# A two-layer encoder kernel: merging the delta rule's chunk stores and moving the load of its decay rows

## The chip, the core and the metric

The kernel runs on one core of a Trainium2 chip. The metric is the device time of one execution in microseconds (us). The core has five engines that run at the same time, each with its own instruction stream in a fixed order: TensorE (PE in the profile, with PEld for its weight loads), VectorE (DVE), ScalarE (ACT), GpSimd (POOL) and SyncE (SP). Here SP issues nearly all the transfers (DMAs) between the device memory (DRAM) and the on-chip memory. An instruction whose input is not there holds up everything behind it on its engine.

## The reference, cut to what matters

The reference runs a two-layer encoder on two sequences, `x_prompt` of 2048 tokens ("p" in the kernel's names) and `x_sample` of 1024 tokens ("s"). Each layer projects the normalised input, runs four mixers side by side (attention, gated delta rule, gated linear attention, attention over a memory), and projects their outputs back. The change touches the gated delta rule, which runs forwards and backwards over chunks of 64 tokens:

```
qkv = jax.nn.silu(short_conv_centered(d_qkv, gdn_conv_w))
qb, kb, vb = jnp.split(qkv, 3, axis=-1)
qb, kb, vb = l2_norm(heads(qb, HEAD_DIM)), l2_norm(heads(kb, HEAD_DIM)), heads(vb, HEAD_DIM)
...
b = jnp.cumsum(g, axis=-1)
diff = b[..., :, None] - b[..., None, :]
decay = jnp.where(incl, jnp.exp(jnp.where(incl, diff, 0.0)), 0.0)
kk = jnp.einsum('bhnid,bhnjd->bhnij', k, k)
lower = jnp.where(strict, beta[..., :, None] * kk * decay, 0.0)
t_mat = lower + jnp.eye(CHUNK, dtype=jnp.float32)
sol = lax.linalg.triangular_solve(t_mat, rhs, left_side=True, lower=True)
...
def step(state, inp):
    qd, a, u_c, w_c, kd, cd = inp
    v_new = u_c - jnp.einsum('bhcd,bhde->bhce', w_c, state)
    o = jnp.einsum('bhcd,bhde->bhce', qd, state) + jnp.einsum('bhij,bhje->bhie', a, v_new)
    state = cd[..., None, None] * state + jnp.einsum('bhcd,bhce->bhde', kd, v_new)
    return state, o
```

## The kernel before

**Streams.** `run` merges generators. A main stream holds the projections (`proj`, `outproj`) in the first and third part of the program and attention plus gated linear attention in the others; a side stream, `right`, goes through the delta rule (`gdn`) of both sequences and layers, and through some of the mixers of the short sequence. `merge` always takes the next step from the stream whose clock stands lowest, where each `yield` says what its step counts (7000 for a chunk tile, 5200 for a projection's tile). A scheduler of the framework then orders the instructions of each engine by priority and by its own model of the chip, so the order on every engine is fixed when the kernel is built.

**The delta rule.** Groups of 1024 tokens go through `gdn_rows` (decay sums and gates, written to the DRAM tensor `rows`), `gdn_chunks`, `gdn_inv` (inverse of the 32 by 32 diagonal blocks, on VectorE) and, when the sequence's groups are through, `gdn_scan`. There are six groups in the program: one a layer of the short sequence, two a layer of the long one. The change is in `gdn_chunks` and in the two that read what it stores.

**`gdn_chunks`.** A group has four blocks of 256 tokens with two tiles of 128 each: 24 blocks and 48 tiles in all. A block first makes v, q and k (the loop over `m`): `raw` is loaded, convolved into `c`, passed through silu with `e`, and for q and k normalised by way of the matmul at L749, `y` and `u`; the result is `qk`. Then each tile

- loads `rb`, the decay and gate rows, copied to 64 partitions at a time (two DMAs of 256 KB, as pieces of 512 bytes),
- copies k into the block-diagonal `kbd` (ScalarE), multiplies k with k and q (L776), and transposes k and v (L779, L780),
- makes `eb = exp(rb)` on ScalarE (L144 is the helper's line, so tile names tell the instructions apart), `dt` from `rb` and `eb` on GpSimd and ScalarE, and from them the pieces of `cm` and `lt`, the lower triangle,
- stores `cm` (one DMA of 772 KB to `cmb`), and `lt` in twelve DMAs of 16 KB: eight with the 32 by 32 diagonal blocks to `lu`, four with the blocks that join them to `off`.

**Buffers.** A tile with two buffers can be written while the last one is still being read; with one buffer the next writer waits. Before, `rb`, `dt`, `eb`, `lt`, `cm`, `e` and `y` have two each, `u` one.

**SP.** All loads and stores of all streams stand in SP's one order. What the projections need (`whi` and `wlo`, 1 MB of weights each) stands in it between the chunks' loads and stores.

Of the kernel before, what the change touches and what calls it, by code (L numbers as in the profile page):

```python
# [16 lines left out]
P = 128  # L17
# [18 lines left out]
HALF = 32  # L36
# [34 lines left out]
class Kern:  # L71
# [641 lines left out]
    def gdn_chunks(self, X, L, g, pp):  # L713
        nc, I = self.nc, self.I
        wide = 2
        with self.tc.tile_pool(name=self.nm("gc"), bufs=1, side="right") as cp:
            mk = lambda shape, tag, bufs=1: self.t(cp, shape, tag, bufs=bufs)
# [3 lines left out]
            for x in kbds:  # L721
                nc.gpsimd.memset(x, 0.0)
            for b in range(g * 1024, g * 1024 + 1024, 256):
                qk = mk([P, 2, 2, 256], "qk", 2)
                vT = mk([P, 2, 256], "vT", 2)
                for m in range(3):
                    raw = mk([P, 2, 258], "raw", 2)
# [8 lines left out]
                    c, e = mk([P, 2, 256], "c", 2), mk([P, 2, 256], "e", wide)  # L736
                    for h in range(2):
                        w = lambda i: cw[:, m * 2 + h, i:i + 1]
# [10 lines left out]
                    nc.tensor.matmul(out=ps, lhsT=self.blk, rhs=e)  # L749
                    y, u = mk([P, 2, 256], "y", wide), mk([P, 2, 256], "u")  # L750
                    self.act(y, ps, AF.Ln, bias=self.eps)
# [3 lines left out]
                    f = 0.125 if m == 0 else 1.0  # L755
# [3 lines left out]
                    yield 4500  # L759
                for tt in range(2):  # L760
                    T = b // P + tt
                    rb = mk([P, 2, 2, 2, P], "rb", wide)
                    kbd = kbds[T % 2]
                    for i in range(2):
                        r = slice(i * 64, i * 64 + 64)
                        self.copy(kbd[r, :, :, r], qk[r, :, 0, tt * P:(tt + 1) * P].rearrange("p h (c t) -> p h c t", c=2))
                    for i in range(2):
                        r = X.rows[g, i].rearrange("w (d h c) t -> (w d h) (c t)", d=2, h=2)[:, (T % 8) * P:(T % 8) * P + P]
                        self.ld(rb[i * 64:i * 64 + 64].rearrange("p w d h x -> p (w d h) x"), r.partition_broadcast(64))
                    rows = lambda w, d: rb[:, w, d].rearrange("p h (c t) -> p c h t", c=2)  # L770
# [7 lines left out]
                    for hp in range(2):  # L778
                        nc.tensor.transpose(out=ptk[:, 0, hp], in_=qk[:, hp, 0, tt * P:(tt + 1) * P], identity=self.ident)  # L779
                        nc.tensor.transpose(out=ptk[:, 1, hp], in_=vT[:, hp, tt * P:(tt + 1) * P], identity=self.ident)  # L780
                    cm = mk([P, 1544], "cm", 2)
                    kv = cm[:, 516:1028].rearrange("p (a c h t) -> p a c h t", a=2, c=2, h=2)
                    for c in range(2):
                        for i in range(2):
# [3 lines left out]
                            else:  # L788
                                nc.vector.tensor_copy(out=o, in_=x)
                    dt, lt, eb = mk([P, 2, 4, 64], "dt", wide), mk([P, 2, 4, 64], "lt", 2), mk([P, 2, 2, 2, 64], "eb", wide)  # L790
                    self.act(eb.rearrange("p d h c t -> p d h (c t)"), rb[:, 0], AF.Exp)
# [14 lines left out]
                    self.st(X.cmb[T], cm)  # L806
                    lu = X.lu[T // 8].rearrange("(d x i) (p j t) -> d i p x j t", d=2, i=2, p=2, j=HALF)
                    x0 = (T % 8) * 4
                    for i in range(2):
                        for p in range(2):  # L810
                            r = slice(i * 64 + p * HALF, i * 64 + p * HALF + HALF)
                            for d in range(2):
                                self.st(lu[d, i, p, x0:x0 + 4].rearrange("x j t -> j x t"), lt[r, d, :, p * HALF:p * HALF + HALF])
                            self.st(X.off[T, p, i], lt[r, p, :, (1 - p) * HALF:(1 - p) * HALF + HALF])
                    yield 7000

    def gdn_inv(self, X, g):

        nc = self.nc
        with self.tc.tile_pool(name=self.nm("gi"), bufs=1, side="right") as ip:  # L820
            fl = lambda x: x.rearrange("p q a b -> p (q a b)")
            U, Y = (self.t(ip, [P, 2, HALF, HALF], n) for n in "UY")
            tmp = self.t(ip, [P, 2 * (HALF // 2) ** 2], "t")
            self.ld(fl(U)[0:64], X.lu[g][0:64])
            self.ld(fl(Y)[64:128], X.lu[g][64:128])
            self.copy(fl(U)[64:128], fl(Y)[64:128, ::-1])
            nc.gpsimd.memset(Y, 0.0)
            nc.gpsimd.memset(Y.rearrange("p q a b -> p q (a b)")[:, :, ::HALF + 1], 1.0)
            for b in range(HALF - 1, 0, -1):
                w = HALF - b  # L830
                t = tmp[:, 0:2 * b * w].rearrange("p (q a c) -> p q a c", q=2, c=w)
                self.vtt(t, b_last(U[:, :, 0:b, b], w), b_at(Y[:, :, b, b:], 2, b), ALU.mult)
                self.vtt(Y[:, :, 0:b, b:], Y[:, :, 0:b, b:], t, ALU.subtract)
                yield 400 + 4 * b * w
            self.copy(fl(U)[64:128], fl(Y)[64:128, ::-1])
            self.st(X.xt[g][0:64], fl(Y)[0:64])
            self.st(X.xt[g][64:128], fl(U)[64:128])
            yield 1500
# [22 lines left out]
    def gdn_scan(self, X, pp):  # L861
        nc = self.nc
        NT = X.S // P
        with self.tc.tile_pool(name=self.nm("gs"), bufs=1, side="right") as cp:
# [14 lines left out]
            def prep(d, T, it):  # L879
                g, x0 = T // 8, (T % 8) * 4  # L880
                cm = mk([P, 1028], "cm", SB_)
                self.ld(cm, X.cmb[T][:, d * 516:d * 516 + 1028])
                cd, qd, at, kv = ((0, 4, 260, 516), (1024, 768, 512, 0))[d]
                v4 = lambda o: cm[:, o:o + 256].rearrange("p (x t) -> p x t", x=4)
                xt = X.xt[g].rearrange("(d x i) (p j t) -> d i p x j t", d=2, i=2, p=2, j=HALF)
                xb, nb = xtb[it % SB_], nbd[d]
                for i in range(2):
                    for p in range(2):
                        r = slice(i * 64 + p * HALF, i * 64 + p * HALF + HALF)
                        self.ld(xb[r, :, r], xt[d, i, p, x0:x0 + 4].rearrange("x j t -> j x t"))  # L890
                    a, o = i * 64 + d * HALF, i * 64 + (1 - d) * HALF
                    self.ld(nb[a:a + HALF, :, o:o + HALF], X.off[T, d, i])
                kvi, ka = mk([P, 4, P], "kvi", KB_), mk([P, 4, P], "ka", KA)
# [178 lines left out]
    def seq(self, nm, S, x, y, mc0):  # L1072
        X = Seq()
        X.nm, X.S, X.x, X.y, X.mc0, X.delta_ready, X.mixed, X.units_done = nm, S, x, y, mc0, (-1, 0), set(), 0
        NT, NG = S // P, S // 1024
        for n, shape in (("h", (S, D)), ("qT", (256, S)), ("kT", (P, S)), ("v", (S, P)), ("gaT", (256, S)), ("mqT", (256, S)),
                         ("gmT", (256, S)), ("dT", (768, S)), ("halo", (1, 768)), ("gd", (S, 256)), ("lqkT", (256, S)), ("lv", (S, 256)),
                         ("gl", (S, 256)), ("smT", (NG, 48, 1024)), ("yT", (D, S)), ("rows", (NG, 2, 2, 64, 64)),
                         ("cmb", (NT, P, 1544)), ("lu", (NG, P, 2048)), ("xt", (NG, P, 2048)), ("off", (NT, 2, 2, HALF, 4, HALF))):
            setattr(X, n, self.dram(nm + n, shape))  # L1080
        return X
# [163 lines left out]
```

## Time and profile before

| what | us |
|---|---|
| median of 3 runs | 5534.79 (5528.48 to 5540.68) |
| the profiled execution, its own time | 5524.39 |
| its span, first to last instruction | 5522.6 |
| TensorE busy in it | 4762.8 (86%) |
| VectorE, ScalarE, GpSimd busy | 3184.6, 2287.8, 1862.9 |
| `gdn_chunks` runs in | 215 to 430, 1337 to 1545, 1632 to 1830, 2300 to 2540, 3698 to 3890, 4120 to 4316 |

The busy time of an engine counts its arithmetic, not its waits. TensorE's clock is granted by the chip at one of two levels, 2.4 GHz (1.00 in the rows) or 1.2 GHz (0.50); a mean between them says how the stretch was shared. Of the six stretches of chunks, the fourth lies beside attention, the others beside projections.

### The profile page before, as it was taken

To read this page: it belongs to the slowest core of one execution; us is meant where nothing else is said; L and a number is where in the kernel's file an instruction comes from. 1 tells how busy PE (TensorE), PEld (TensorE's weight loads), DVE (VectorE), ACT (ScalarE), POOL (GpSimd) and SP (SyncE) were. 2 spreads that over 40 slices of the span, in tenths; PEclk is the share of its full clock that TensorE was granted. 3 is DMA by queue.
4 is the path that set the end of the run, shared out by engine and by line. 5 is a ranking of instruction groups with operands and counts; after the bars stand their busy time and mean duration, and the time that the engine had idled before them with its cause. 6 is when DMAs were issued, how large, how long until landed. Compare 5 with 4: busy or idle time off the path is not lost. (4 is left out here: it accounts for less than half of the span.)

```text
span 5522.6 us, 76962 instructions
## 1 busy us (share of the span) xinstructions
PE 4762.8 (86%) x26984; PEld 3660.2 (66%) x26984; DVE 3184.6 (58%) x6175; ACT 2287.8 (41%) x5027; POOL 1862.9 (34%) x1836
## 2 busy tenths in 40 slices
PE   6878999899678798578889899986887899999998
PEld 5758888667576698434455478665865866555887
DVE  4465254554556525577876665626426478877553
ACT  4344233434425244454444433424325255554332
POOL 0232121043413323266656220324104234665222
PEclk8989999999888899778999999998988999999999
DMA  5556343433575544332222246334534543232674
GB/s 188 165 175 200 117 136 129 141 110 123 158 228 159 194 154 114 79 92 56 72 67 74 72 165 212 109 109 116 188 117 123 171 130 94 62 94 56 244 261 152
DMA packets 558154, 746.61 MB, mean 135 GB/s; under 512 B 227200, under 2 KB 420486, under 8 KB 528584
## 3 DMA queue, kind: packets, MB, share of 16 engines
q1 hardware_dynamic: 557768, 741.69, 42.8%
q8 instruction: 214, 3.51, 0.3%
q14 instruction: 172, 1.41, 0.1%
HBM read 490.41 MB, written 251.07 MB: 134 GB/s over the span
## 5 line engine op out<-in xcount | busy, mean ns | idle before, releaser
L278 PE MATMUL b<-whi,xhi 128*128 128x256 f32 x3520 | 1017.2, 290 | 65.1 <-ACT stg L147 34.4
L278 PE MATMUL b<-wlo,xhi 128*128 128x256 f32 x3520 | 1012.1, 288 | 0.0
L278 PE MATMUL b<-whi,xlo 128*128 128x256 f32 x3520 | 1004.6, 288 | 0.1
L153 POOL TENSOR_TENSOR acc<-acc,p 128x512 f32<-128x512 f32 x544 | 738.0, 1357 | 419.9 <-ACT p L144 386.4
L278 PEld LDWEIGHTS b<-whi,xhi 128*128 128x128 f32 x3520 | 685.5, 195 | 100.4 <-issue 40.1
L278 PEld LDWEIGHTS b<-whi,xlo 128*128 128x128 f32 x3520 | 680.9, 195 | 23.5 <-issue 14.7
L278 PEld LDWEIGHTS b<-wlo,xhi 128*128 128x128 f32 x3520 | 685.5, 195 | 16.3 <-issue 12.4
L565 DVE TENSOR_REDUCE mx<-b 128x1 f32<-128x512 f32 (+1 forms) x832 | 501.8, 622 | 287.4 <-PE b L564 283.5
L278 PE MATMUL b<-xhi,whi 128*128 128x512 f32 x1472 | 598.0, 407 | 51.9 <-DMA whi<-hi_wg 23.0
L278 PE MATMUL b<-xlo,whi 128*128 128x512 f32 x1472 | 591.8, 402 | 0.6 <-DVE xlo L150 0.6
L144 ACT ACTIVATE p<-b 128x512 f32<-128x512 f32 x736 | 417.4, 595 | 419.3 <-PE b L635 402.5
L278 PE MATMUL b<-xhi,wlo 128*128 128x512 f32 x1472 | 589.7, 401 | 0.0
L634 PE MATMUL b<-qh,kst 128*128 128x512 f32 x736 | 345.2, 471 | 48.7 <-DVE mx L565 36.3
L564 PE MATMUL b<-kst,qh 128*128 128x512 f32 (+1 forms) x832 | 342.5, 443 | 41.6 <-ACT p L144 25.5
L278 PEld LDWEIGHTS b<-xhi,whi 128*128 128x128 f32 x1472 | 278.8, 189 | 138.3 <-ACT stg L147 28.2
L621 PE MATMUL b<-p,vst 128*64 128x512 f32 x1280 | 361.3, 635 | 3.9 <-ACT p L144 3.7
L278 PEld LDWEIGHTS b<-xhi,wlo 128*128 128x128 f32 x1472 | 277.1, 188 | 78.3 <-issue 13.2
L278 PEld LDWEIGHTS b<-xlo,whi 128*128 128x128 f32 x1472 | 278.5, 189 | 73.9 <-issue 9.4
L635 PE MATMUL b<-qlm,kh 68*128 68x512 f32 x736 | 299.6, 420 | 19.4 <-DVE qlm L150 19.1
L634 PEld LDWEIGHTS b<-qh,kst 128*128 128x128 f32 x736 | 145.0, 197 | 219.3 <-DVE mx L565 99.4
L564 PEld LDWEIGHTS b<-kst,qh 128*128 128x128 f32 x832 | 159.6, 200 | 174.5 <-ACT p L144 65.7
L147 ACT ACTIVATE stg<-b 128x512 f32<-128x512 f32 (+2 forms) x212 | 112.7, 545 | 322.9 <-PE b L278 240.9
(249 smaller groups left out, 9152.3 us busy)
## 6 DMA issues: line engine op xcount, KB each, us to landing
whi<-hi_wg SPq DMA_DIRECT2D x48, 1024.0 KB
wlo<-lo_wg SPq DMA_DIRECT2D x48, 1024.0 KB
cm<-pcmb SPq DMA_DIRECT2D x64, 514.0 KB
whi<-hi_wout SPq DMA_DIRECT2D x28, 1024.0 KB
wlo<-lo_wout SPq DMA_DIRECT2D x28, 1024.0 KB
pcmb<-cm SPq DMA_DIRECT2D x32, 772.0 KB
h<-in_wg_dram SPq DMA_DIRECT2D x48, 512.0 KB
hi_wg<-whi SPq DMA_DIRECT2D x24, 1024.0 KB
```

The source lines that it names most:

```text
L144: self.nc.scalar.activation(out=out, in_=in_, func=func, **k)
L147: self.nc.scalar.activation(out=out, in_=in_, func=AF.Copy)
L153: self.nc.gpsimd.tensor_tensor(out=out, in0=a, in1=b, op=op)
L278: self.nc.tensor.matmul(out=out, lhsT=a, rhs=b, start=(i == 0), stop=(i == len(terms) - 1))
L564: nc.tensor.matmul(out=ps, lhsT=qh[:, qt * P:(qt + 1) * P], rhs=kst[:, lb * LB:(lb + 1) * LB])
L565: nc.vector.tensor_reduce(out=mx[:, qt, lb:lb + 1], in_=ps, axis=AX.X, op=ALU.max)
L621: return nc.tensor.matmul(out=pv[r], lhsT=vst[:, lt, 0:64], rhs=p, start=(lt < 2), stop=(lt >= NL - 2))
L634: nc.tensor.matmul(out=s, lhsT=kst[:, lt * P:(lt + 1) * P], rhs=qh, start=True, stop=False)
L635: nc.tensor.matmul(out=s, lhsT=kh1[0:68, lt * P:(lt + 1) * P], rhs=qlm[0:68], start=False, stop=True)
```

## The change

Each chunk tile stores five pieces instead of thirteen. `lt` becomes the last 512 columns of `cm`, so that the joining blocks go out with the store of `cm` (1028 KB) and the scan reads them from `cmb`; the tensor `off` goes. The order of the lanes in `lu` and `xt` is changed so that one store of 32 KB (256 pieces of 128 bytes) takes a diagonal block of both directions, four stores a tile. `rb` is loaded for both tiles at the head of its block, ahead of `raw`, and has three buffers; to make room, `y` and `eb` go from two buffers to one.

```
@@ gdn_chunks
+            def rb_load(T):
+                rb = mk([P, 2, 2, 2, P], "rb", 3)
+                for i in range(2):
+                    r = X.rows[g, i].rearrange("w (d h c) t -> (w d h) (c t)", d=2, h=2)[:, (T % 8) * P:(T % 8) * P + P]
+                    self.ld(rb[i * 64:i * 64 + 64].rearrange("p w d h x -> p (w d h) x"), r.partition_broadcast(64))
+                return rb
...
                 vT = mk([P, 2, 256], "vT", 2)
+                rbs = [rb_load(b // P + tt) for tt in range(2)]
                 for m in range(3):
...
-                    y, u = mk([P, 2, 256], "y", wide), mk([P, 2, 256], "u")
+                    y, u = mk([P, 2, 256], "y"), mk([P, 2, 256], "u")
...
-                for tt in range(2):
+                for tt, rb in enumerate(rbs):
                     T = b // P + tt
-                    rb = mk([P, 2, 2, 2, P], "rb", wide)
                     kbd = kbds[T % 2]
...
-                    for i in range(2):
-                        r = X.rows[g, i].rearrange("w (d h c) t -> (w d h) (c t)", d=2, h=2)[:, (T % 8) * P:(T % 8) * P + P]
-                        self.ld(rb[i * 64:i * 64 + 64].rearrange("p w d h x -> p (w d h) x"), r.partition_broadcast(64))
...
-                    cm = mk([P, 1544], "cm", 2)
+                    cm = mk([P, 2056], "cm", 2)
...
-                    dt, lt, eb = mk([P, 2, 4, 64], "dt", wide), mk([P, 2, 4, 64], "lt", 2), mk([P, 2, 2, 2, 64], "eb", wide)
+                    dt, eb = mk([P, 2, 4, 64], "dt", wide), mk([P, 2, 2, 2, 64], "eb")
+                    lt = cm[:, 1544:2056].rearrange("p (d x t) -> p d x t", d=2, x=4)
...
-                    lu = X.lu[T // 8].rearrange("(d x i) (p j t) -> d i p x j t", d=2, i=2, p=2, j=HALF)
-                    x0 = (T % 8) * 4
+                    lu = X.lu[T // 8].rearrange("(n i m) (p j t) -> n i p m j t", i=2, m=8, p=2, j=HALF)
                     for i in range(2):
                         for p in range(2):
                             r = slice(i * 64 + p * HALF, i * 64 + p * HALF + HALF)
-                            for d in range(2):
-                                self.st(lu[d, i, p, x0:x0 + 4].rearrange("x j t -> j x t"), lt[r, d, :, p * HALF:p * HALF + HALF])
-                            self.st(X.off[T, p, i], lt[r, p, :, (1 - p) * HALF:(1 - p) * HALF + HALF])
+                            self.st(lu[T % 8, i, p].rearrange("m j t -> j m t"), lt[r, :, :, p * HALF:p * HALF + HALF].rearrange("j d x t -> j (d x) t"))
@@ gdn_inv
-            self.ld(fl(U)[0:64], X.lu[g][0:64])
-            self.ld(fl(Y)[64:128], X.lu[g][64:128])
+            lanes = lambda a, d: a[g].rearrange("(n d x) f -> d n x f", d=2, x=4)[d]
+            self.ld(fl(U)[0:64], lanes(X.lu, 0))
+            self.ld(fl(Y)[64:128], lanes(X.lu, 1))
...
@@ gdn_scan, prep
+                off = X.cmb[T][:, 1544:2056].rearrange("(i p j) (d x q t) -> i d p q j x t", i=2, p=2, d=2, x=4, q=2)
...
-                        self.ld(xb[r, :, r], xt[d, i, p, x0:x0 + 4].rearrange("x j t -> j x t"))
+                        self.ld(xb[r, :, r], xt[i, p])
...
-                    self.ld(nb[a:a + HALF, :, o:o + HALF], X.off[T, d, i])
+                    self.ld(nb[a:a + HALF, :, o:o + HALF], off[i, d, d, 1 - d])
```

The orders on the engines move with it. The first place is SP at the end of a block, here the first block of the long sequence's first group in layer 0. Before, 26 stores of the two tiles stand ahead of the `rb` loads of the second block (the last ten are shown):

```order
L135 DMA pcmb<-cm_11135 128x1544
L135 DMA plu<-lt_11141 32x4x32 x2
L135 DMA poff<-lt_11141 128x1x32
L135 DMA plu<-lt_11141 32x4x32 x2
L135 DMA poff<-lt_11141 128x1x32
L135 DMA plu<-lt_11141 32x4x32 x2
L135 DMA poff<-lt_11141 128x1x32
L135 DMA plu<-lt_11141 32x4x32 x2
L135 DMA poff<-lt_11141 128x1x32
L135 DMA rb_11488<-prows 64x8x128 x2
L135 DMA rb_11700<-prows 64x8x128 x2
L135 DMA raw_11903<-pdT 128x2x258
```

In the change, the same place of SP's order, where `rb_11163` belongs to the second tile of the second block and `rb_11723` to the first tile of the third:

```order
L135 DMA pcmb<-cm_10858 128x2056
L135 DMA plu<-cm_10858 32x8x32 x4
L135 DMA rb_11163<-prows 64x8x128 x2
L135 DMA pgd<-stg_12715 128x2x256
L135 DMA pcmb<-cm_11052 128x2056
L135 DMA plu<-cm_11052 32x8x32 x4
L135 DMA rb_11723<-prows 64x8x128 x2
```

The loads moved from behind both tiles' stores to behind each tile's five stores, and a block or half a block further ahead of their use. The second place is SP at the head of the group, where `raw` is the conv's input. Before:

```order
L135 DMA cw_10774<-in_conv_dram 128x18
L135 DMA raw_10782<-pdT 128x2x257
L135 DMA raw_10842<-pdT 128x2x257
L135 DMA rb_10914<-prows 64x8x128 x2
L135 DMA rb_11120<-prows 64x8x128 x2
L135 DMA pgd<-stg_12663 128x2x256
```

And in the change, with a third tile's rows (`rb_11160`) as well:

```order
L135 DMA cw_10700<-in_conv_dram 128x18
L135 DMA rb_10708<-prows 64x8x128 x2
L135 DMA rb_10711<-prows 64x8x128 x2
L135 DMA raw_10714<-pdT 128x2x257
L135 DMA raw_10774<-pdT 128x2x257
L135 DMA rb_11160<-prows 64x8x128 x2
```

Here the four `rb` DMAs moved from behind the first two `raw` loads to ahead of them. The third place is ScalarE at the second block's exponents (`eb`). Before, they stand around the copies of k to `kbd` of the same block:

```order
L144 ACTIVATE e_11476<-e_11476 128x512
L144 ACTIVATE eb_11510<-rb_11488 128x512
L147 ACTIVATE kbd_1974_10776<-qk_11250 64x4x64 x2
L147 ACTIVATE kbd_1975_10777<-qk_11250 64x4x64 x2
L144 ACTIVATE eb_11722<-rb_11700 128x512
L144 ACTIVATE e_11476<-e_11476 128x512
```

In the change, the first of them (`eb_11420`) stands between the copies to `cm` of the first block's two tiles:

```order
L147 ACTIVATE cm_10858<-b_1994_10853 64x2x128 x2
L144 ACTIVATE gt_12716<-gt_12716 128x512
L144 ACTIVATE e_11169<-c_11168 128x512
L144 ACTIVATE e_11276<-c_11275 128x512
L144 ACTIVATE eb_11420<-rb_11160 128x512
L147 ACTIVATE cm_11052<-b_2021_11047 64x2x128 x2
L144 ACTIVATE e_11276<-e_11276 128x512 x2
L147 ACTIVATE stg_12766<-b_2244_12741 128x512
```

The second block's own copies to `kbd` stand eighteen rows behind it, so the exponent moved ahead of them by that many.

## Rows read from the trace of the kernel before

**Rows 1.** The page: its span.
```profile
span 5522.6 us, 76962 instructions
```

**Rows 2.** Windows of the six stretches of chunks: two of them, and the sum.
```profile
core 0: us, PE busy (x) PEld busy (x) DVE busy (x) ACT busy (x) POOL busy (x), PEclk, DMA share, GB/s
1337.00:1545.00 208.00, 148.78 (x997) 136.39 (x996) 111.32 (x204) 101.15 (x206) 82.72 (x82) 0.84 0.55 165
2300.00:2540.00 240.00, 154.03 (x528) 76.65 (x528) 170.35 (x281) 120.42 (x262) 147.96 (x136) 0.75 0.35 82
sum 1249.00, PE 861.16 PEld 672.98 DVE 769.76 ACT 614.59 POOL 550.77; mean PE 143.53 PEld 112.16 DVE 128.29 ACT 102.43 POOL 91.80
```

**Rows 3.** Window of an inversion, just behind a stretch of chunks.
```profile
4316.00:4384.00 68.00, 68.00 (x471) 63.65 (x470) 42.83 (x73) 17.26 (x25) 10.81 (x12) 1.00 0.56 182
```

**Rows 4.** Waits over the span: us in total, times, longest us.
```profile
ACT eb L144 <- DMA rb<-prows: 204.9, 32, 12.2
ACT eb L144 <- DMA rb<-srows: 76.2, 16, 12.2
```

**Rows 5.** Timeline of ScalarE (start, us, ..., idle before): second, third block.
```profile
1409.05 0.61 ACT L144 ACTIVATE e<-e 128x512 f32<-128x512 f32 x1
1419.49 0.63 ACT L144 ACTIVATE eb<-rb 128x512 f32<-128x512 f32 x1 [9.82 <-DMA rb<-prows]
1426.51 0.63 ACT L144 ACTIVATE eb<-rb 128x512 f32<-128x512 f32 x1 [4.79 <-DMA rb<-prows]
...
1461.83 0.63 ACT L144 ACTIVATE eb<-rb 128x512 f32<-128x512 f32 x1 [12.22 <-DMA rb<-prows]
```

**Rows 6.** Timeline of SP's DMA issues at the same place.
```profile
1409.51 0.56 SPq L135 DMA_DIRECT2D poff<-lt  x1
1410.11 2.65 SPq L135 DMA_DIRECT2D rb<-prows  x4
1417.08 2.65 SPq L135 DMA_DIRECT2D whi<-hi_wg  x1
```

**Rows 7.** Windows, sum of the 36 stalls at eb in later blocks.
```profile
sum 225.24, PE 122.58 PEld 97.64 DVE 76.22 ACT 0.08 POOL 49.67; mean PE 3.40 PEld 2.71 DVE 2.12 ACT 0.00 POOL 1.38
```

**Rows 8.** Windows, sum of the 12 stalls in first blocks.
```profile
sum 55.88, PE 15.70 PEld 14.53 DVE 29.64 ACT 0.03 POOL 8.24; mean PE 1.31 PEld 1.21 DVE 2.47 ACT 0.00 POOL 0.69
```

**Rows 9.** Timelines of SP, ScalarE and VectorE in a group's first block.
```profile
4124.75 0.96 SPq L135 DMA_DIRECT2D raw<-pdT  x2
4125.75 2.68 SPq L135 DMA_DIRECT2D rb<-prows  x4
...
4128.05 0.91 ACT L144 ACTIVATE c<-raw,cw 128x256 f32<-128x256 f32 x2 [2.40 <-DMA raw<-pdT]
4141.36 0.63 ACT L144 ACTIVATE eb<-rb 128x512 f32<-128x512 f32 x1 [5.49 <-DMA rb<-prows]
4141.90 0.61 ACT L144 ACTIVATE e<-c 128x512 f32<-128x512 f32 x1
...
4132.24 0.88 DVE L741 SCALAR_TENSOR_TENSOR c<-raw,cw,c 128x256 f32<-128x256 f32 x2
```

**Rows 10.** Instructions on tile lt: ns min/median/max.
```profile
L135 SPq DMA_DIRECT2D plu<-lt x256: 302/452/1963, 1392.8 to 4316.3; - x128
L135 SPq DMA_DIRECT2D poff<-lt x128: 555/556/1427, 1393.1 to 4316.8; - x128
```

**Rows 11.** Timelines of ScalarE and GpSimd at the two y of a block.
```profile
1398.71 0.67 ACT L144 ACTIVATE y<-b,c_eps 128x512 f32<-128x512 f32 x1
...
1401.25 1.30 POOL L153 TENSOR_TENSOR u<-u,y 128x512 f32<-128x512 f32 x1 [1.26 <-DVE u L756]
1403.42 1.04 POOL L153 TENSOR_TENSOR u<-y 128x512 f32<-128x512 f32 x1 [0.87 <-DVE qk L150]
```

**Rows 12.** Waits of TensorE for the end of the q and k chain, and for weights.
```profile
PE b L779 <- DVE qk L150: 108.2, 11, 18.3
PE b L278 <- DMA whi<-hi_wg: 23.0, 2, 12.9
```

More of the change, by code (lines that the diff above doesn't have):

```diff
@@ L835, in gdn_inv @@
             self.copy(fl(U)[64:128], fl(Y)[64:128, ::-1])
-            self.st(X.xt[g][0:64], fl(Y)[0:64])
-            self.st(X.xt[g][64:128], fl(U)[64:128])
+            self.st(lanes(X.xt, 0), fl(Y)[0:64])
+            self.st(lanes(X.xt, 1), fl(U)[64:128])
             yield 1500
@@ L879, in prep @@
             def prep(d, T, it):
-                g, x0 = T // 8, (T % 8) * 4
+                g = T // 8
                 cm = mk([P, 1028], "cm", SB_)
@@ L884, in prep @@
                 v4 = lambda o: cm[:, o:o + 256].rearrange("p (x t) -> p x t", x=4)
-                xt = X.xt[g].rearrange("(d x i) (p j t) -> d i p x j t", d=2, i=2, p=2, j=HALF)
+                xt = X.xt[g].rearrange("(n i d x) (p j t) -> n d i p j x t", i=2, d=2, x=4, p=2, j=HALF)[T % 8, d]
+                off = X.cmb[T][:, 1544:2056].rearrange("(i p j) (d x q t) -> i d p q j x t", i=2, p=2, d=2, x=4, q=2)
                 xb, nb = xtb[it % SB_], nbd[d]
@@ L1078, in seq @@
                          ("gl", (S, 256)), ("smT", (NG, 48, 1024)), ("yT", (D, S)), ("rows", (NG, 2, 2, 64, 64)),
-                         ("cmb", (NT, P, 1544)), ("lu", (NG, P, 2048)), ("xt", (NG, P, 2048)), ("off", (NT, 2, 2, HALF, 4, HALF))):
+                         ("cmb", (NT, P, 2056)), ("lu", (NG, P, 2048)), ("xt", (NG, P, 2048))):
             setattr(X, n, self.dram(nm + n, shape))
```

## The prediction

> **What bounds the kernel now.** I read the page first: the span is 5522.6 us [rows 1], and TensorE is the busiest engine. So a change off TensorE pays only where TensorE stands still, and the next view was the windows, to see in which stretches that is. In the six stretches of chunks it is: 1249.00 us long together, TensorE busy 861.16 us of them [rows 2], so idle 387.84 us or 31%. Its granted clock there lies between 0.75 and 0.84 in the two stretches shown, the lowest and the highest of the six; right behind a stretch of chunks, where VectorE inverts and TensorE only projects, TensorE is busy 68.00 us of 68.00 at a clock of 1.00 [rows 3]. The reader is to see that it is the chunks that take TensorE's time away, twice: it waits, and it then runs partly at 1.2 GHz.
>
> Who makes it wait is in the view of waits: ScalarE waits at `eb` for the load of `rb` 204.9 and 76.2 us, 48 times, once for every tile [rows 4]. A timeline of one block shows how. ScalarE reaches `eb` at about 1409.7, sits idle 9.82 us until the first tile's rows land at 1419.49, and 4.79 us more for the second's [rows 5]. SP had issued the four loads at 1410.11, right behind the last of the previous block's stores [rows 6]; they landed 9.4 and 16.4 us later. Behind `eb` on ScalarE stand the copies to `kbd`, for which TensorE waits, and the evacuations of the projections' PSUM banks. So the chain is: 26 stores on SP, then the loads, then ScalarE, then TensorE.
>
> How much of that TensorE feels is read from windows laid on exactly the 48 stalls. In the 36 of the second to fourth blocks, 225.24 us, TensorE is busy 122.58 us [rows 7]: it loses 102.66 us, and in the rest it still has projections ahead in its order. In the 12 of the first blocks, 55.88 us, it is busy 15.70 us [rows 8]: it loses 40.18 us.
>
> **The change part by part.** The sum is made against the profiled execution's own time, 5524.39 us.
>
> *Rows loaded ahead, later blocks (A).* The order on SP now puts a load of `rb` behind five stores, half a block or a whole block ahead of its use. A block takes about 42 us here (`eb` at 1419.49, the next block's at 1461.83 [rows 5]), and the loads landed 16.4 us after their issue at the most [rows 5, 6], so half a block covers it. The order on ScalarE moves `eb` ahead of the `kbd` copies, so the exponents are made when ScalarE has room. I take the whole 102.66 us of TensorE's idle time: −103. The bounds are 0, if the next wait on the same chain takes its place, and −103; the upper end is nearer since both ScalarE's wait and its cause go.
>
> *Clock (B).* A stretch with 31.1% idle time has 0.80 (between the two of rows 2), one with none has 1.00 [rows 3]. An estimate along that line: idle falls to 387.84 − 103 + 29 = 314 of 1175 us, 26.7%, and the clock rises to 1 − 0.20 × 26.7 / 31.1 = 0.83. TensorE's 861 us then become 861 × 0.80 / 0.83 = 830: −31. Bounds 0 and −61 (twice that).
>
> *First blocks (C).* There is no earlier time to load in: `rows` has only just been written, and the four loads now stand ahead of `raw`. Before, `raw` was issued at 4124.75 and convolved at 4128.05, 3.3 us later; the `rb` loads took from 4125.75 to 4141.36, 15.6 us, and `e`, the next step of the conv, came behind them at 4141.90, 17.2 us after the start [rows 9]. In the change `raw` comes behind the loads: 15.6 + 3.3 = 18.9 us to the conv's start, and 5.1 us that the conv takes on ScalarE and VectorE until `e` can follow (4128.05 to 4133.12 [rows 9]), 24.0 us instead of 17.2. That is 6.8 us a group, 41 us in six; at the 72% of ScalarE's stall that TensorE lost there (40.18 / 55.88) it is +29. Bounds 0 (TensorE has projections ahead of the first conv's matmul) and +58 (the third tile's load, also ahead of later `raw`s, costs as much again).
>
> The Trainium skill bears on this term: "DMA: Bandwidth & Descriptors", section "Anatomy of one DMA — SWDGE (gpsimd) path", fits 2.0 us plus bytes / 436 GB/s to a DMA that GpSimd issues, an estimate of 2.6 us for 256 KB. By it the loads would delay `raw` by some 3 us, C would be about 0 and the sum 29 us lower; the row's 15.6 us for four of these loads, copied from the same few DRAM rows to 64 partitions, says otherwise, and I go by the row.
>
> *One buffer for `y` and `eb` (D).* The second Ln to `y` ran at 1398.71; with one buffer it waits for GpSimd's `u<-u,y` of the first, which ended at 1402.55, and with 0.67 + 0.63 us for Ln and Exp `y` is there at 1403.85. GpSimd's next `u` started at 1403.42 anyway, since `u` has one buffer already [rows 11]. So the chain loses 0.43 us a block, 10 us in 24; half of it on TensorE: +5. What is queued behind the waiting Ln is ScalarE's 3.8 us (1398.71 to 1402.55); 24 of those are 92 us, and at the share that TensorE lost in the later stalls (102.66 / 225.24 = 46%) the upper bound is +42. For `eb`, the second tile's Exp waits until GpSimd and VectorE have read the first's, but the new order puts a dozen and more ScalarE instructions between two `eb`: 0.
>
> *Fewer stores (E).* Twelve stores of `lt` took SP 8 × 0.452 + 4 × 0.556 = 5.84 us a tile [rows 10]. Four with twice the pieces take between 0.302 us (the shortest of rows 10) and 0.66 us (a load of `rb`, 2.65 / 4 in rows 6, with twice as many pieces again), 1.2 to 2.6 us: SP gains 3.2 to 4.6 us a tile, 155 to 220 us in 48. Most of it is already in A, since it is why `rb` is late. Beyond that, two tiles' gain at each of six group ends brings the inversion forward, some 40 us in all on the side stream, while TensorE has projections to do [rows 3]: a fifth, −8 (bounds 0 and −40).
>
> The wider `cm` store, `lt`'s new place in it, the strided lanes in the inversion and the joining blocks read from `cmb` I cost at nothing: the store is read again only by the scan, a group or more later, and the joining blocks move the same 128-byte pieces as before, loaded beside the scan's first matmuls. Without that cover, 192 of these loads at even 0.2 us each would be 38 us.
>
> Sum: −103 − 31 + 29 + 5 − 8 = −108, and 5524.39 − 108 = 5416.4. The median of the runs shown lies 10.4 us above the profiled execution (5534.79 − 5524.39): **5427 us**.
>
> **Rivals.**
> - *More goes than the stalls themselves.* TensorE also waits 108.2 us at L779 for the end of the q and k chain [rows 12]; GpSimd makes a link of that chain and was itself held by `rb` through `dt`. If half goes, −54: 5373. For it speaks the order, which now has `dt` and `eb` out of the chain's way; against it, that part of these waits lies inside the 48 stalls already counted.
> - *The next wait takes over.* With one `y`, ScalarE stands at the second Ln instead of at `eb`, the upper bound of D, and C is at its upper bound: −108 + 37 + 29 = −42: 5493. For it: ScalarE is still one queue for the chunks and the projections' banks. Against it: `u` already enforced most of that wait.
> - *Nothing, the change does not do what it says.* If the `rb` loads land as late as before, because SP reaches them no sooner, A, B and E are 0 and C falls away: 5535. Against it: eight of thirteen stores stand no longer ahead of them.
> - *Slower.* The `rb` loads wait on SP for a buffer, and a wait there holds the weights behind it. `whi` was issued 7 us behind `rb` [rows 6], and TensorE waited for such weights 23.0 us in all [rows 12]. If each of the 20 blocks beside projections got its 2 MB later by more than 108 / 20 = 5.4 us, and TensorE had nothing else, the gain would be gone; at 8 us it would be −108 + 160 = +52: 5587. Against it: in the new order the load stands right behind the store of a `cm` that waits for the same GpSimd instruction, so it waits for nothing further.
>
> **How the numbers follow.** 0.2%, some 11 us, is about what a measurement of this kernel can tell from no change. The forecast (5395 to 5465) has a chance of 0.52, the larger gain (below 5395) 0.20, the next wait (5465 to 5524) 0.15, nothing (5524 to 5546) 0.06, slower 0.07. So faster 0.87, same 0.06, slower 0.07. The range's low end is the sum with B at twice its size (−30), E at its bound (−32) and C and D at 0 (−34): 5331, so 5330. Its high end takes half of A away (+51) and D at its bound (+37): 5515. It leaves out the last two cases and the edges, some 0.17.
>
> **What would show it right or wrong.** A: ScalarE's waits at `eb` for `rb` fall from 281 us to under 60, nearly all in first blocks, and the idle time of TensorE in the six stretches from 388 to about 314 us. B: the clock there rises to 0.82 or more. C: in first blocks ScalarE waits for `raw` some 10 us, where it waited 2 to 3. D: a wait of ScalarE at `y` for GpSimd appears. E: SP issues 328 DMAs fewer. The prediction is wrong if TensorE's idle time stays while the `rb` waits go, or if weights come late.

## The result and the profile after

The changed kernel takes 5366.65 us (median of 4 runs, 5355.76 to 5368.73), the kernel before in the same comparison 5531.64 us: a ratio of 0.9708 (95% interval 0.9692 to 0.9723), 2.9% faster. Ratios are taken from undisturbed runs; the kernel with raw first below has one disturbed run of 11846 us, without which its median is 5359.19 and not 5363.08. The forecast was 5427, with 5395 to 5465 as the likeliest case's own range; the time lies 28 us below that, among the times of the rival "more goes than the stalls themselves" (5373), and inside the range of 5330 to 5515.

The page of the changed kernel, its span and engines:

```profile
span 5364.8 us, 76462 instructions
PE 4721.5 (88%) x26984; PEld 3637.5 (68%) x26984; DVE 3187.6 (59%) x6175; ACT 2285.1 (43%) x5027; POOL 1858.8 (35%) x1836
```

Against [rows 1] the span is 157.8 us shorter. TensorE's busy time fell from 4762.8 to 4721.5, 41.3 us, with the same 26984 matmuls. That is the clock: its mean over the span is 0.936, before 0.924, and averaged over TensorE's busy time alone 0.955 against 0.948, which makes 39 of the 41.3 us. The other 116.6 us are idle time of TensorE. The six stretches of chunks, each from the issue of the conv weights to the issue of the inversion's load `Y`, answer to [rows 2] (two of six, and the sum; columns as there):

```profile
1297.10:1477.90 180.80, 146.58 (x938) 133.41 (x937) 114.65 (x196) 100.02 (x191) 81.58 (x82) 0.87 0.62 193
2214.60:2432.40 217.80, 141.25 (x523) 70.02 (x524) 168.31 (x274) 120.48 (x254) 154.19 (x137) 0.80 0.38 97
sum 1092.30, PE 800.72 PEld 625.69 DVE 753.98 ACT 595.87 POOL 555.77; mean PE 133.45 PEld 104.28 DVE 125.66 ACT 99.31 POOL 92.63
```

Cut at the same two events, the stretches before are 1238.0 us long with 385.6 idle (the windows of [rows 2] are rounded, and 11 us longer together). Now they are 1092.3, with 1092.3 − 800.7 = 291.6 idle: 145.7 us of the 157.8 went inside them. The waits of the changed kernel over the span (us, times, longest), against [rows 4, 12]:

```profile
PE b L341 <- DVE stg L150: 113.4, 24, 13.4
ACT y L144 <- POOL u L153: 48.5, 17, 9.5
ACT eb L144 <- POOL cm L153: 43.7, 13, 7.1
PE b L783 <- DVE qk L150: 41.6, 14, 9.9
ACT eb L144 <- DMA rb<-prows: 32.5, 6, 8.8
ACT c L144 <- DMA raw<-pdT: 21.5, 5, 5.8
DVE cm L799 <- DMA plu<-cm: 17.1, 5, 7.0
ACT eb L144 <- DMA rb<-srows: 12.4, 2, 8.6
```

The wait of `eb` for `rb` fell from 281.1 us in 48 stalls to 44.9 in 8, all but 5.6 us in first blocks. TensorE's wait for the q and k chain (L779, now L783) fell from 108.2 to 41.6. Two waits that the one buffer brings are new (`y` and `eb` for GpSimd, 92 us), and TensorE's wait at L341 (transposes of rope tiles, beside the chunks) rose from 42.9 to 102.1 us in the stretches. In the group of [rows 5, 6], ScalarE's two `eb` of the third block and SP's issues of rows behind the second block's stores:

```profile
1391.42 0.94 SPq L135 DMA_DIRECT2D rb<-prows  x1
1392.52 1.24 SPq L135 DMA_DIRECT2D pcmb<-cm  x1
1393.81 4.84 SPq L135 DMA_DIRECT2D plu<-cm  x4
1398.69 3.34 SPq L135 DMA_DIRECT2D rb<-prows  x3
...
1388.30 0.63 ACT L144 ACTIVATE eb<-rb 128x512 f32<-128x512 f32 x1
1404.91 0.63 ACT L144 ACTIVATE eb<-rb 128x512 f32<-128x512 f32 x1 [3.82 <-DMA rb<-prows]
```

The first tile's `eb` waits for nothing: its rows were issued at 1363.57 and 1367.63, 20 us and more ahead. Of the second tile's two loads one (1391.42) still stands behind one tile's five stores and the other (the first of the three from 1398.69) behind both tiles'; that costs 3.82 us here, where the third block's two `eb` waited 12.22 and 5.75 us before. The second block's two `eb`, at 1350.94 and 1373.62, wait for no rows.

### The profile page after: what moved, and what is told of

Read it like the earlier page. It is cut to its first block, busy times and chain, and to the rows that moved or that the text cites. A ratio compares the mean times of both kernels' runs of the same rounds, so it can differ in the third digit from the quotient of the medians.

```text
span 5364.8 us, 76462 instructions
## 1 busy us (share of the span) xinstructions
PE 4721.5 (88%) x26984; PEld 3637.5 (68%) x26984; DVE 3187.6 (59%) x6175; ACT 2285.1 (43%) x5027; POOL 1858.8 (35%) x1836
## 4 chain that ended last, share of the span: by engine, by line
PE 35%; DVE 10%; DMA 5%; ACT 3%; issue 2%; POOL 1%; SPq 1%; DVEq 0%; ACTq 0%; POOLq 0%
PE b L278 16%; PE b L621 4%; PE b L634 2%; PE b L635 2%; PE b L564 2%; DVE mx L565 2%; PE b L630 1%; DVE qlm L150 1%; PE b L1061 1%; DVE c L749 1%; PE b L1042 1%; SPq L135 1%; PE b L912 1%; PE b L916 1%; PE b L592 1%
## 5 line engine op out<-in xcount | busy, mean ns | idle before, releaser
L153 POOL TENSOR_TENSOR acc<-acc,p 128x512 f32<-128x512 f32 x544 | 736.2, 1353 | 441.1 <-ACT p L144 409.4
L144 ACT ACTIVATE p<-b 128x512 f32<-128x512 f32 x736 | 416.7, 595 | 413.6 <-PE b L635 400.2
L634 PE MATMUL b<-qh,kst 128*128 128x512 f32 x736 | 341.4, 465 | 51.4 <-DVE mx L565 41.6
L564 PEld LDWEIGHTS b<-kst,qh 128*128 128x128 f32 x832 | 159.0, 199 | 159.9 <-ACT p L144 55.4
```

What stands on the lines that cost most here:

```text
L144: self.nc.scalar.activation(out=out, in_=in_, func=func, **k)
L153: self.nc.gpsimd.tensor_tensor(out=out, in0=a, in1=b, op=op)
L564: nc.tensor.matmul(out=ps, lhsT=qh[:, qt * P:(qt + 1) * P], rhs=kst[:, lb * LB:(lb + 1) * LB])
L634: nc.tensor.matmul(out=s, lhsT=kst[:, lt * P:(lt + 1) * P], rhs=qh, start=True, stop=False)
```

## The experiments

All twelve are compared with the kernel before by the same ratio. This table puts their profiled runs beside each other; the last four are told at the end. A stretch is cut in three: from its first issue (`cw`, or `rb` where that goes first) to the first block's first `kbd` copy, from there to the fourth block's, and from there to the inversion's load ("tail"); all are sums over the six stretches. "rb" is ScalarE's wait at `eb` for `rb` in later blocks.

| kernel | ratio (95%) | stretches, us | start, blocks, tail | PE idle in them | rb |
|---|---|---|---|---|---|
| before | 1 | 1238.0 | 254, 829, 154 | 385.6 | 225.2 |
| one `y`, one `eb` | 0.9991 (0.998 to 1.0002) | 1226.3 | 250, 822, 155 | 367.3 | 174.6 |
| loads ahead, 13 stores | 0.9938 (0.9925 to 0.9952) | 1219.0 | 274, 788, 157 | 338.8 | 116.8 |
| 5 stores, loads in the tile | 0.9866 (0.9852 to 0.9879) | 1173.7 | 253, 786, 135 | 330.2 | 164.7 |
| changed, two `rb`, `y`, `eb` | 0.9824 (0.9811 to 0.9838) | 1156.0 | 275, 759, 121 | 308.6 | 166.5 |
| changed, 8 stores added | 1.0008 (1.0 to 1.0017) | 1250.2 | 275, 803, 172 | 373.5 | 132.5 |
| loads lifted, 13 stores | 0.9818 (0.9806 to 0.9831) | 1156.2 | 284, 712, 160 | 288.3 | 0 |
| loads lifted, 5 stores | 0.9842 (0.9826 to 0.9858) | 1147.2 | 283, 745, 119 | 312.9 | 0 |
| **changed** | 0.9708 (0.9692 to 0.9723) | 1092.3 | 287, 695, 110 | 291.6 | 5.6 |
| changed, raw first | 0.9698 (0.9678 to 0.9719) | 1091.4 | 250, 724, 118 | 255.3 | 0 |
| changed, `dt` behind `cm` | 0.9734 (0.9716 to 0.9752) | 1125.2 | 291, 688, 147 | 274.3 | 10.2 |
| lifted, 5 stores, `dt` behind `cm` | 0.9834 (0.9817 to 0.985) | 1180.4 | 303, 735, 143 | 311.3 | 0 |
| the same with raw first | 0.9759 (0.9739 to 0.9779) | 1118.5 | 254, 734, 131 | 285.9 | 0 |
| lifted, `lt` apart, 6 stores | 0.9757 (0.9735 to 0.9779) | 1114.0 | 283, 716, 116 | 286.6 | 0 |

Outside the stretches each of these kernels spends 4242 to 4285 us of its span, so most of what an edit does is read from the stretches.

**Loads ahead alone.** The kernel before with `rb_load` at the block's head, three `rb`, one `y` and `eb`:

```
+                rbs = [rb_load(b // P + tt) for tt in range(2)]
...
-                    for i in range(2):
-                        r = X.rows[g, i]...
```

> The kernel before with the decay rows loaded at the head of the block (three buffers of rb, one of y and of eb), and all thirteen stores a tile left as they were. If the place of the load is what counts (my steps A and B), ScalarE's waits at eb for rb fall from 281 us to under 80 and most of the 158 to 165 us of the full change is here: 5390 to 5425 us. If the stores' time on SP is what counts, they still stand ahead of everything else and the gain is at most a third: 5475 us or more.

Measured 5489.01 us, 0.6%: the theory that the place where the load is written is the main part falls. SP of this run, at the end of a first block, and ScalarE behind it:

```profile
1395.85 0.33 SPq L135 DMA_DIRECT2D plu<-lt  x1
...
1411.52 0.56 SPq L135 DMA_DIRECT2D poff<-lt  x1
1412.12 2.64 SPq L135 DMA_DIRECT2D rb<-prows  x4
...
1421.74 0.63 ACT L144 ACTIVATE eb<-rb 128x512 f32<-128x512 f32 x1 [8.86 <-DMA rb<-prows]
```

The loads are written at the head of the block, but on SP the 26 stores, 16.2 us of them, still go ahead, and the second block's second `eb` waits 8.86 us, as its first did before (9.82 in [rows 5]). The first tile's rows, loaded into the third buffer, are in time. Half of the later blocks' wait is left.

**Five stores alone.** The changed kernel with the loads back in the tile and two `rb`, `y` and `eb`:

```
-                rbs = [rb_load(b // P + tt) for tt in range(2)]
...
+                    for i in range(2):
+                        r = X.rows[g, i]...
```

> The changed kernel with the decay rows loaded where they were, in the tile (two buffers of rb, y and eb), so that only the five stores remain. By my steps rb is issued some 7 us sooner after a block's last store (two tiles at 3.2 to 4.6 us), which takes most of the first tile's wait and little of the second's: about 100 of 225 us of ScalarE's wait, 46% of it TensorE's, and a third as much from the clock, so about -60: 5470 us (5440 to 5500). If the stores alone are the cause: 5390 to 5425 us. If they only fill time on SP that nobody waits for: 5520 to 5540 us.

Measured 5450.62 us, −1.3%, in the range of the prediction's steps (5440 to 5500). Only 60 us of the 225 us wait went, but the tail is 19 us shorter. The two parts alone give −34 and −74 us by their ratios, together −161: each leaves most of a wait that goes only when both are there (225 to 117, to 165, and with both to 5.6).

**The third buffer.** The changed kernel with two `rb`, and `y` and `eb` with two again:

```
-                rb = mk([P, 2, 2, 2, P], "rb", 3)
+                rb = mk([P, 2, 2, 2, P], "rb", 2)
...
-                    y, u = mk([P, 2, 256], "y"), mk([P, 2, 256], "u")
+                    y, u = mk([P, 2, 256], "y", wide), mk([P, 2, 256], "u")
...
```

> The changed kernel with two buffers of rb instead of three, and two of y and eb again instead of one. In the trace after, ScalarE waits 48.5 us at y and 43.7 us at eb for GpSimd, the single buffers' price. If these waits count (step D), and half a block ahead is enough for rb, 10 to 40 us come back: 5327 to 5357 us. If the waits are covered and half a block is enough: 5360 to 5373 us. If the third buffer is what brings rb in time: 5400 us or more, with ScalarE's waits for rb back over 120 us.

Measured 5428.22 us. With two buffers a load cannot go ahead of the tile that still reads its buffer: from the issue of the second load of a tile's rows to the start of its `eb` the median is 9.1 us, against 9.2 in the kernel before and 22.2 in the changed one, and the wait is back at 166.5 us. The third `rb` is worth 1.2%, net of the one `y` and one `eb` that pay for its room; what these cost by themselves is the next run.

**One `y` and one `eb`.** The kernel before with these two on one buffer each:

```
-                    y, u = mk([P, 2, 256], "y", wide), mk([P, 2, 256], "u")
+                    y, u = mk([P, 2, 256], "y"), mk([P, 2, 256], "u")
...
```

> The kernel before with only y and eb on one buffer each; stores and the place of the loads as before. Theory (single buffers put a chain of waits on ScalarE, which the whole change pays too: 48.5 us at y and 43.7 us at eb in its profile, some of it shown at TensorE): 5535 to 5560 us, with new ScalarE waits at y for GpSimd's u and at eb for GpSimd's cm of 40 to 100 us together. Rival (the waits only take the place of waits that ScalarE has there anyway): 5520 to 5534, no difference from before.

Measured 5511.01 us, where the kernel before took 5516.17: no difference, although the wait is there (`ACT y L144 <- POOL u L153` 36.2 us, 14 times). It takes the place of other waits: the later blocks' wait for `rb` is 50.6 us shorter. In the changed kernel that wait is gone, and what one `y` and one `eb` cost there no run shows.

**Raw first.** The changed kernel with the first block's `rb` loads behind its first two `raw`:

```
-                rbs = [rb_load(b // P + tt) for tt in range(2)]
+                rbs = [rb_load(b // P + tt) for tt in range(2)] if b % 1024 else None
...
+                    if rbs is None and m == 1:
+                        rbs = [rb_load(b // P + tt) for tt in range(2)]
```

> The changed kernel, but in a group's first block rb is loaded behind the raw loads of q and k, as before the change; the other blocks are unchanged. In the trace after, the first convolution of a group starts some 15 us after the head of the group instead of 4, and the first copies to kbd come 4 to 7 us later than before. If that costs (step C), 10 to 30 us come back: 5337 to 5357 us. If TensorE has projections enough to cover it, no change: 5360 to 5373 us. If rb is then late again for the first tile, slower: 5375 us or more.

Measured 5363.08 us. By the ratios (0.9698 and 0.9708, with overlapping intervals) the branch without a difference held, and its page shows where the gain went:

```profile
span 5361.3 us, 76525 instructions
PE 4752.1 (89%) x26984; PEld 3657.6 (68%) x26984; DVE 3193.3 (60%) x6175; ACT 2284.4 (43%) x5027; POOL 1859.2 (35%) x1836
```

The first blocks start 37 us earlier in sum, and TensorE idles 34 us less over the span (609.2 against 643.3); but the same 26984 matmuls take 30.6 us longer. The granted clock, averaged over TensorE's busy time alone, is 0.950 against 0.955, which is 28 of these 30.6. Why the clock was lower is not shown. It belongs in part to this one execution: by the mean over the span the kernel's four times lie at 0.934 to 0.941, the profiled one at the lowest, and the changed kernel's at 0.935 to 0.938.

**Eight stores back.** The changed kernel with eight more stores of 16 KB a tile, into a tensor that nothing reads (extra work, the output is untouched):

```
+                            for d in range(2):
+                                self.st(X.off[T, d, p, i], lt[r, d, :, (1 - p) * HALF:(1 - p) * HALF + HALF])
```

> The changed kernel with eight extra stores of 16 KB a tile into a DRAM tensor that nobody reads, so thirteen stores a tile again, everything else as changed. They stand ahead of the next block's rb loads in SyncE's order again. Theory (the number of issues on SyncE's queue is what the five stores save, and the loads come late behind them): 5460 to 5500 us, later-block rb waits 80 to 130 us. Rival (the gain came from what is stored, the pieces of the layout or the loads of the inversion and scan that read it, not from the number of issues): 5365 to 5400.

Measured 5523.68 us: the whole gain is gone, more than the theory expected. So it is the stores themselves that count; layout and reads stayed as changed, and that rival falls. The waits for `rb` are back (150.7 and 24.0 us), the blocks take 803 us and the tail 172. What of the stores counts is not parted here: beside eight issues they add 128 KB and 1024 pieces a tile, and they hold `cm`, for which VectorE now waits 51 us, where it waited 23.

**Loads lifted, thirteen stores.** The first run's kernel with a scheduling priority for the loads, which puts them ahead of most of the 26 stores in SP's order:

```
+                with self.lifted(LIFT):
+                    rbs = [rb_load(b // P + tt) for tt in range(2)]
```

> As the first experiment (all thirteen stores a tile, three rb buffers, loads written at the block's head), but the loads get a scheduling priority that puts them ahead of 22 or more of the 26 small stores in SyncE's order. Theory (what held the first experiment at 5489 us was its place: 26 stores stood ahead of the loads in SyncE's order): ScalarE's waits at eb for rb in later blocks fall from 116.8 us to under 20, chunk stretches from 1219 us to 1130 to 1175, time 5400 to 5445. Rival (the stores' own time on the queue and in the DMA engines matters, wherever the loads stand): 5470 to 5490 with the rb waits gone all the same and other waits in their place.

Measured 5418.03 us: with all thirteen stores left, the loads' place on SP gives 1.2% over the first run, and the later blocks wait for `rb` no more. What still parts its stretches from the changed kernel's is mostly the tail, 160 against 110 us. TensorE idles no longer in them (288.3 us, in the changed kernel 291.6), but 26 us longer in the six inversions behind, from the load `Y` to the last store of `xt` (62.0 against 35.8). SP at the end of the last stretch of this run:

```profile
4194.73 0.32 SPq L135 DMA_DIRECT2D plu<-lt  x1
...
4209.49 0.56 SPq L135 DMA_DIRECT2D poff<-lt  x1
...
4211.47 0.50 SPq L135 DMA_DIRECT2D U<-plu  x1
```

And of the changed kernel at the same place:

```profile
4147.87 0.32 SPq L135 DMA_DIRECT2D pcmb<-cm  x1
...
4152.09 3.73 SPq L135 DMA_DIRECT2D plu<-cm  x4
...
4158.32 0.55 SPq L135 DMA_DIRECT2D U<-plu  x1
```

From the first store to the inversion's load it is 16.7 us with thirteen stores a tile and 10.5 with five. The inversion's load stands behind the last tiles' stores, and nothing in the chunks is left to do there.

**Loads lifted, five stores.** The same two lines in the changed kernel:

> The changed kernel with the rb loads at a scheduling priority that puts them ahead of the large store of the tile before. Theory (in later blocks only 5.6 us of rb waits are left, so the place has nothing more to give; in first blocks the loads stand ahead of the first raw already): 5355 to 5375 us, no difference from the changed kernel's 5366. Rival (an rb that is there earlier shortens the chunk stretches still): under 5350.

Measured 5430.77 us, 1.4% slower than the changed kernel by the ratios: neither branch. The blocks take 50 us longer. Two waits that grew could be the cause, and each got a run. GpSimd's timeline of this run, in the group of [rows 5]:

```profile
1386.28 1.19 POOL L153 TENSOR_TENSOR dt<-rb,ppb 128x256 f32<-128x256 f32 x2 [4.89 <-DMA rb<-prows]
...
1396.64 1.27 POOL L153 TENSOR_TENSOR u<-u,y 128x512 f32<-128x512 f32 x1 [6.80 <-DVE u L765]
```

And its waits over the span, at ScalarE's `dt` and at VectorE's first write to a tile's `cm`:

```profile
ACT dt L144 <- POOL dt L153: 76.0, 19, 8.1
DVE cm L800 <- DMA plu<-cm: 66.7, 11, 15.2
DVE cm L800 <- DMA slu<-cm: 17.3, 4, 6.0
```

**`dt` behind `cm`.** GpSimd's `dt` may only stand behind `cm<-qk,eb`, so that it doesn't wait for `rb` ahead of `u`; in the lifted kernel, in the changed kernel, and in the lifted kernel with raw first:

```
+                        with self.tc.issue_after(mul.ins):
+                            self.gtt(x4(dt[:, d]), rows(0, d), b_last(pp["b"][:, d, T * 2:T * 2 + 2], 64), ALU.subtract)
```

> The lifted loads of the run before (five stores, loads ahead of the large store) together with the dt subtractions placed behind cm<-qk,eb. Theory (the lifted loads lost 1.4% because the scheduler, with rb due earlier, put dt ahead of u in GpSimd's order, where it waited 4.9 us for rb while u, ScalarE's y and the next qk stood behind): 5350 to 5390 us, ScalarE's waits at dt for GpSimd from 76 us to under 35, chunk stretches from 1147 to 1080 to 1115. Rival (they lost it because the loads wait at the head of SyncE's order and hold raw and the stores): 5410 to 5440 still.

> The changed kernel with GpSimd's two dt subtractions of a tile placed in its order behind the product cm<-qk,eb of the same direction, so that a dt that waits for rb no longer stands ahead of the next block's u; loads as changed. Theory (in the changed kernel 129 us of GpSimd's waits are dt for rb, and part of them hold u and so y on ScalarE, 48.5 us): 5330 to 5360 us. Rival (these waits lie where GpSimd has nothing else to do): 5360 to 5375, no difference from the changed kernel.

> All three together: raw first in the first block of a group, the later blocks' loads lifted, dt behind cm<-qk,eb. If each of these removes a wait that the others leave, 5310 to 5350 us, under the changed kernel by 0.3 to 1%. If TensorE's clock or the next wait takes it back, as in the run with raw first alone (idle time down 34 us, busy time up 31), 5350 to 5375.

The lifted kernel stays at 5428.74 us, with ScalarE's wait at `dt` down from 76 to 6 us. But another has taken its place, since the product that `dt` now follows waits for the stores of `cm`:

```profile
ACT eb L144 <- POOL cm L801: 52.8, 19, 10.8
POOL cm L801 <- DMA plu<-cm: 42.0, 8, 9.5
```

The first was 9.8 us in the lifted kernel, so by this run alone the `dt` theory neither stands nor falls. The changed kernel with it takes 5372.62, its rival's branch, with ScalarE's waits at `y`, `eb` and `dt` for GpSimd down from 115 to 53 us: nothing is gained by that, though a tail that is 37 us longer may hide some of it. The three together take 5381.10, slower than the changed kernel and in neither branch's favour.

**`lt` apart.** The lifted kernel with `lt` in a buffer pair of its own, so that `cm` is held by one store instead of five:

```
-                    cm = mk([P, 2056], "cm", 2)
+                    cm = mk([P, 1544], "cm", 2)
...
-                    self.st(X.cmb[T], cm)
+                    self.st(X.cmb[T][:, 0:1544], cm)
+                    self.st(X.cmb[T][:, 1544:2056], lt.rearrange("p d x t -> p (d x t)"))
```

> The lifted loads with five stores once more, but lt has a buffer pair of its own again (of the same size together: cm 1544 and lt 512 wide instead of cm 2056) and is stored into the wide DRAM rows by a store of its own, so six stores a tile; cm's buffer is then held by one store and not by five. Theory (the lifted loads lost 1.4% against the changed kernel because the stores, now behind the loads, land later and hold cm: VectorE waits 84 us at cm for them, where it waited 23): VectorE's waits at cm for stores under 20 us, chunk stretches from 1147 to 1090 to 1115, time 5360 to 5390. Rival (those waits cost TensorE nothing, and the loss has another cause): 5415 to 5435 still, with the waits gone.

Measured 5385.38 us, stretches 1114.0: the theory's time. But its wait didn't go:

```profile
DVE cm L799 <- DMA pcmb<-cm: 65.2, 11, 9.1
DVE cm L799 <- DMA scmb<-cm: 13.0, 4, 6.3
```

VectorE waits 78 us at `cm`, now for the one store, instead of 84, and ScalarE's wait at `dt` is 75.7 us, as it was. So most of the time came back with both waits in place. Neither of them explains that part, and why the lifted loads lose stays open. With the loads lifted, five stores are no faster than thirteen (0.9842 against 0.9818), and six with `lt` apart are by 0.6%: what fewer stores give depends on the rest of the order. Of the runs no kernel beats the changed one; raw first equals it.

## Why the prediction was right, and where its sizes were off

The mechanism held: the chain from SP's stores over the `rb` loads and ScalarE to TensorE was the one to cut, and by its own signs the `rb` waits fell below 60 us, the clock in the stretches rose (0.813 to 0.843, weighted by length), waits at `y` appeared, and SP issued 384 stores fewer (the prediction said 328 DMAs; eight a tile in 48 tiles are 384). One sign fell short: in first blocks ScalarE waits 5 to 6 us for `raw`, not some 10. The sum was 50 us short (−108 against −157.8). The time came out near the rival's 5373 by other terms than the rival's: of the 50 us, 21 are C, 12 E and 10 B, and only the small rest lies in A and D and outside the terms. Term by term:

- **A, rows loaded ahead (−103):** TensorE's idle time in the stretches fell 94 us; with the 8 us that first blocks lost (C), that is 102, the size predicted. It is not made of what the step added up alone, though. 66.6 us came from the q and k chain's wait at L779, which the prediction kept for its rival (−54) and of which 41.4 us lay inside A's 36 stalls; the waits for `kbd` and for the projections' banks, which the step named, fell by some 50; and the wait at L341 grew by 59. That last wait grows in every run of the table, by 41 us with one `y` and one `eb` and no change of time, so it is not shown to be A's price. That A needs both edits was said only in passing under E; the runs show it as the main thing: loads alone −0.6%, stores alone −1.3%, both −2.9%. That holds for the scheduler's own order: lifted ahead of thirteen stores, the loads alone bring −1.8%.
- **B, clock (−31):** −41.3 over the span. In the stretches the term was right: TensorE's busy time there, times what the granted clock lacks to 1.00, is 113.6 us before and 86.6 now, −27. Most of the rest lies outside them, where the term counted nothing.
- **C, first blocks (+29):** the step that was mis-sized. The first blocks do start later, in sum 287 − 254 = 32 us of stretch (41 were worked out). The charge of 72% for TensorE failed: its idle time up to the first `kbd` rose only from 118.6 to 126.8 us; in the rest it had other work, the term's lower bound. The last first block, against [rows 9]:

```profile
3987.80 2.67 SPq L135 DMA_DIRECT2D rb<-prows  x4
3990.51 3.94 SPq L135 DMA_DIRECT2D raw<-pdT  x2
...
3996.69 0.63 ACT L144 ACTIVATE eb<-rb 128x512 f32<-128x512 f32 x1 [7.98 <-DMA rb<-prows]
4002.39 0.91 ACT L144 ACTIVATE c<-raw,cw 128x256 f32<-128x256 f32 x2 [5.07 <-DMA raw<-pdT]
...
4009.51 0.63 ACT L144 ACTIVATE e<-c 128x512 f32<-128x512 f32 x1
```

  The conv starts 14.6 us after the loads' issue (18.9 predicted) and `e` 21.7 us after (24.0 predicted, 17.2 before). The first pair of rows is there 8.9 us after its issue. The Trainium skill's fit ("DMA: Bandwidth & Descriptors", section "Anatomy of one DMA — SWDGE (gpsimd) path") is for a DMA that GpSimd issues and gives an estimate of 2.6 us for 256 KB. These loads, issued by SP, do not agree with it: 8.9 us for the two. Raw first removed the late start and no time.
- **D, one buffer (+5):** not measured in the changed kernel, where its wait is there, 92 us on ScalarE; in the kernel before the same edit alone cost nothing (0.9991). The rival "the next wait takes over" falls with the time.
- **E, fewer stores (−8):** mis-sized the other way. The tail got 44 us shorter, where some 40 were worked out; in the inversions behind it TensorE's idle time fell by 20 us (55.4 to 35.8), not 8. That the tail did this is not shown: with one `y` and one `eb` alone, and no shorter tail, it is 42.6. Eight stores put back undid the whole change, so the stores may cost more beyond the loads they delay than was taken; the pairs of runs above put that between nothing and 1.1%.

"Nothing" fell with the first time. So did "slower": TensorE's wait for the weights of [rows 12] is gone from the stretches, not grown. With the loads further ahead still, in the lifted kernel, 1.4% is lost again, but no run shows that it is by this rival's mechanism.

## What to carry to other kernels

A load that is written earlier is not issued earlier while other issues stand ahead of it in its queue: look at the queue's order and at the number of buffers, which had both to change here. Two such edits can be worth more than their sum, as they were here. Count a stall's price in TensorE's idle time, not by a share read elsewhere: first blocks that came 32 us later cost 8 us of it, and tails shorter by 44 us saved none inside them (6.9 us idle before, 16.4 now) and at most 20 in the inversions behind. And idle time that goes need not be time that goes: one profiled execution with 34 us less of it took as long, with 28 us more from a lower clock.

## What the runs showed of the hardware

- Issuing small stores took SP long: 24 stores of 16 KB and two `cm` stores 16.2 us, and 384 stores fewer moved the time by 1.3% even with the loads left where they were.
- A store of 32 KB in 256 pieces took SP little longer than one of 16 KB in 128: median 0.564 us for `plu<-cm` in the changed kernel, against 0.452 and 0.556 us [rows 10].
- Re-orderings that no named wait accounts for move this kernel by near 1%: the lifted kernels with `lt` in `cm` and apart from it differ by 0.85%, with all but the same waits at `cm` (84 and 78 us) and `dt` (76.0 and 75.7). A term of some 20 us in a forecast lies inside that, and so do the 0.6% of the loads alone; the 2.9% of the change, and their loss with eight stores back, do not.
